# A hybrid GLA and RWKV-7 layer on one core: transfers planned to end later, the first 12 split weights read where they are made, row statistics spread by products with a repeated column

## The chip, the core and the metric

The kernel runs on one core of a Trainium2 chip. The core's engines each run their own queue in order: TensorE (PE in the profile, its weight loads PEld) multiplies matrices, VectorE (DVE) and ScalarE (ACT) work on tiles element by element, GpSimd (POOL) does the rest of such work, and SyncE (SP) issues the transfers, which 16 DMA engines carry out. Engines wait for each other by semaphores. The metric is the device time of one launch in microseconds (us).

## What is computed

One layer of a hybrid decoder: 4096 positions of width 1024, in float32. A projection of the normalised input feeds 4 heads of gated linear attention (GLA) and 8 heads of an RWKV-7 recurrence; their outputs, gated, go through one output projection, a residual add and a last normalisation.

```python
def _hybrid_layer(x, ...):
    h = _rmsnorm(x, norm_w)
    u = (h @ w_in).astype(f32)
    gla_u, rwkv_u = u[..., :GLA_IN], u[..., GLA_IN:]
    ...
    o = _gla_chunked(q, k, v, log_a)
    o = o * lax.rsqrt(jnp.mean(o * o, axis=-1, keepdims=True) + NORM_EPS) * gla_norm_w
    gla_out = o.reshape(B, T, GLA_VW) * jax.nn.silu(gg)
    ...
    y = _rwkv7_scan(r_h, decay, k_h, v_h, kk, a)
    y = (y - mu) * lax.rsqrt(var + RWKV_GN_EPS)
    rwkv_out = (y * rwkv_ln_w + rwkv_ln_b + bonus) * jax.nn.silu(rg)
    merged = jnp.concatenate([gla_out, rwkv_out], axis=-1)
    return x + merged @ w_out

x = _hybrid_layer(x, ...)
return _rmsnorm(x, final_norm_w)
```

## The kernel before

**Tiling.** Positions are taken in 8 blocks of 512 (b), features lie on the 128 partitions. A block needs 29 input weights of 1024 x 128: one for the two low-rank inputs (W_WA), for each of 4 pairs of RWKV heads four (W_R, W_RK, W_RV, W_RG), and 12 for GLA (W_K, W_Q, W_V, W_GG). The output projection has 8 more. Per block, rwkv_ab (L754) projects a pair of heads and builds the matrices of its 8 chunks of 64 positions (tiles De, Do, bk, Nb), rwkv_c (L909) walks the recurrence over the chunks with small products (tiles ch, sv, us, psd), rwkv_d (L951) normalises; gla_proj and gla_pair do GLA; out_block (L1137), and for the last block out_last (L1171), the output. There are 8 x 4 = 32 such RWKV units.

**Split weights.** Each float32 operand is written as a high and a low float16 part, and a product is three float16 products (high by high, high by low, low by high), so one weight costs 24 products of 128x128 by 512 columns. The weights are split on the chip in the first block, in the order of w_order (L581: W_WA, RK, R, then K, Q, then RV, RG, RK, then V, V and so on). split_w (L542) takes the absolute maximum of the raw weight on ACT (its elementwise result goes into the buffer hl, tiles wo, as scratch), spreads it over the partitions by a small product with ident (tile amW), makes a power of two of it on VectorE (tiles pw, scl, invs), and writes the high part on ACT and the low part on VectorE into hl. store_w (L560) stores hl to DRAM (wdr). There are two buffers hl, taken in turn. get_w (L525) loads a weight's two parts from wdr into a pair of tiles, wr for RWKV (4 tiles, so two pairs) or wg for GLA (3 tiles); the first block does so too.

**Row statistics.** A sum over the partitions comes out of stat_mm (L609) as rows: positions 128 g to 128 g + 127 in partition group g of 32. newton (L592) takes the inverse square root on VectorE (tiles nva, nta, nya, nyg, nyc). To spread a row over all partitions, bcast (L613) stores it to DRAM and loads it back repeated. At the two ends of the kernel spread (L625) is used in its place: it clears a tile rk on POOL, copies the four row groups into it on ACT, and multiplies by a constant sel. It is called in the first x_block, in the last rwkv_d and at the end of out_last.

**What sets the order.** Engine calls are recorded, not issued. Streams (generators for x, weights, recurrence and so on) hand their steps to a planner, which accounts each with a cost and builds a graph of steps (put, L196). forward (L230) and backward (L280) then simulate lists on the engines, and the steps are issued in the order of the planned starts. A transfer is planned with 0.63 us on SP's issue, 1.28 us until it starts, its bytes at 360 KB per us, and lag until others may use it: 1.6 us for a read from DRAM, 0.6 us for a write. A step that reuses a tile which a transfer reads follows 0.95 us after it. The output tensor counts as one DRAM tensor, so its stores follow each other in the plan. SP's queue is one for all transfers, and each DMA also waits for the one eight places earlier.

All engine calls go through one helper, so nearly all rows of the profile have its line, L364.

## Time and profile before

| | us |
|---|---|
| runs before: median of 3 | 2439.53 |
| lowest, highest | 2435.34, 2442.73 |
| the profiled execution | 2439.58 |
| its span, first to last instruction | 2437.8 |

The shares of that span: TensorE busy 94%, VectorE 70%, ACT 50%, POOL 35%; DMA engines 47% by the queues' packets. The page cuts the span into 40 slices of about 61 us; in the next lines each digit is the busy share of TensorE in a slice in tenths, then its granted clock, then the DMA engines' busy share.

```profile
PE   6799999999999999999999999999999999999996
PEclk9899999999999999999999999999999999999998
DMA  7775555454334553346433453346533454334431
```

Busy time of an engine does not add up over engines: a part of one engine's time matters where others wait for it. The lines on waits say who waited for whom; the chain follows the last instruction back to what released it.

### The profile page before, as it was taken

To read this page: it belongs to the slowest core of one execution; us is meant where nothing else is said; L and a number is where in the kernel's file an instruction comes from. 1 tells how busy PE (TensorE), PEld (TensorE's weight loads), DVE (VectorE), ACT (ScalarE), POOL (GpSimd) and SP (SyncE) were. 2 spreads that over 40 slices of the span, in tenths; PEclk is the share of its full clock that TensorE was granted. 3 is DMA by queue.
4 is the path that set the end of the run, shared out by engine and by line. 5 is a ranking of instruction groups with operands and counts; after the bars stand their busy time and mean duration, and the time that the engine had idled before them with its cause. 6 is when DMAs were issued, how large, how long until landed. Compare 5 with 4: busy or idle time off the path is not lost.

```text
span 2437.8 us, 54473 instructions
## 1 busy us (share of the span) xinstructions
PE 2292.0 (94%) x20684; PEld 1338.1 (55%) x20684; DVE 1696.4 (70%) x3866; ACT 1226.7 (50%) x3135; POOL 862.1 (35%) x2219
## 2 busy tenths in 40 slices
PE   6799999999999999999999999999999999999996
PEld 2456565455655555555564556555556455655652
DVE  7778778567675686757667667657867567576765
ACT  7456764454544555445544445445545455444342
POOL 3351434424334443335334153342433444323300
PEclk9899999999999999999999999999999999999998
DMA  7775555454334553346433453346533454334431
GB/s 226 241 249 181 169 152 149 111 166 142 90 109 117 171 146 96 97 122 185 120 94 109 136 178 112 99 120 184 137 98 103 122 163 130 109 98 119 143 90 64
DMA packets 278476, 331.91 MB, mean 136 GB/s; under 512 B 131540, under 2 KB 132804, under 8 KB 278212
## 3 DMA queue, kind: packets, MB, share of 16 engines
q1 hardware_dynamic: 278212, 328.42, 46.3%
q8 instruction: 162, 2.65, 0.5%
q14 instruction: 102, 0.84, 0.1%
HBM read 283.26 MB, written 45.05 MB: 135 GB/s over the span
## 4 chain that ended last, share of the span: by engine, by line
PE 48%; DVE 28%; DMA 11%; ACT 7%; issue 3%; SPq 2%; POOL 0%; DVEq 0%; ACTq 0%; POOLq 0%
PE bank L364 41%; PE ch L364 5%; DVE nta L364 3%; DVE bk L364 2%; DVE Nb L364 2%; DMA xr<-in_xT_dram 2%; DMA wdr<-wo 2%; DVE De L364 2%; DVE Do L364 2%; PE y L364 2%; SPq L364 2%; DVE cy L364 1%; DMA rn<-bcda 1%; DVE x L364 1%; ACT wo L364 1%
## 5 line engine op out<-in xcount | busy, mean ns | idle before, releaser
L364 PE MATMUL bank<-x,wr 128*128 128x512 f16 x3264 | 808.7, 381 | 12.1 <-DVE rgs L364 5.3
L364 POOL TENSOR_TENSOR tm<-Tc,f 128x60 f32<-128x60 f32 (+24 forms) x961 | 346.0, 360 | 711.1 <-DMA f<-nd 535.5
L364 PEld LDWEIGHTS <-wr 128*128 128x128 f16 x3264 | 308.0, 100 | 313.2 <-issue 24.7
L364 PE MATMUL bank<-x,wg 128*128 128x512 f16 x1536 | 386.2, 381 | 5.4 <-DMA wg<-wdr 4.8
L364 POOL TENSOR_TENSOR Tc<-Tc,tm 128x60 f32<-128x60 f32 (+24 forms) x961 | 343.8, 358 | 73.7
L364 PE MATMUL bank<-x,wo 128*128 128x512 f16 x1488 | 362.3, 381 | 0.5 <-ACT x L364 0.5
L364 DVE SCALAR_TENSOR_TENSOR sv<-ch,PC,psd 64x64 f32<-64x64 f32 x448 | 126.1, 281 | 207.2 <-PE ch L364 198.7
L364 POOL TENSOR_TENSOR xacc<-xacc,xr 128x512 f32<-128x512 f32 x98 | 132.0, 1347 | 371.2 <-ACT xr L364 224.6
L364 ACT ACTIVATE psd<-sv,PC 64x64 f32<-64x64 f32 x512 | 171.8, 342 | 137.5 <-DVE sv L364 130.8
L364 PEld LDWEIGHTS <-wg 128*128 128x128 f16 x1536 | 145.8, 100 | 154.5 <-issue 10.3
L364 PEld LDWEIGHTS <-wo 128*128 128x128 f16 x1488 | 141.2, 100 | 137.1 <-issue 4.4
L364 PEld LDWEIGHTS <-x 128*128 128x128 f16 x3120 | 188.7, 99 | 31.9 <-issue 12.0
L364 PE MATMUL bank<-wg,x 128*128 128x128 f16 x3072 | 202.7, 221 | 2.3 <-DMA wg<-wdr 1.4
L364 ACT COPY sv<-ch 64x64 f32<-64x64 f32 x512 | 105.0, 205 | 99.0 <-PE ch L364 91.8
L364 ACT ACTIVATE sa<-bank,mu_s 128x512 f32<-128x512 f32 x104 | 71.5, 687 | 130.9 <-PE bank L364 129.7
L364 PEld LDWEIGHTS ch<-us,Nb 128*128 128x128 f32 x512 | 87.7, 190 | 68.8 <-ACT us L364 54.4
L364 ACT COPY us<-ch 128x64 f32<-128x64 f32 x256 | 53.8, 210 | 140.4 <-PE ch L364 138.4
L364 POOL MEMSET Tc<- 32x8 f32 (+1 forms) x160 | 23.9, 150 | 277.1 <-DMA td<-Tc 261.3
L364 PEld LDWEIGHTS ch<-sv,bk 128*128 128x128 f32 x512 | 89.7, 190 | 47.8 <-ACT sv L364 31.8
L364 PE MATMUL ch<-us,Nb 128*128 128x64 f32 x512 | 94.4, 266 | 19.5 <-ACT us L364 17.8
L364 PE MATMUL ch<-sv,bk 128*128 128x128 f32 x512 | 105.5, 288 | 6.5 <-ACT sv L364 6.1
L364 PEld LDWEIGHTS ch<-sv,De 128*64 128x64 f32 x512 | 49.1, 135 | 97.3 <-issue 44.7
(323 smaller groups left out, 4111.0 us busy)
## 6 DMA issues: line engine op xcount, KB each, us to landing
wr<-wdr SPq DMA_DIRECT2D x272, 256.0 KB
wg<-wdr SPq DMA_DIRECT2D x192, 256.0 KB
xr<-in_xT_dram SPq DMA_DIRECT2D x176, 256.0 KB
wo<-wdr SPq DMA_DIRECT2D x128, 256.0 KB
wdr<-wo SPq DMA_DIRECT2D x37, 512.0 KB
f<-nd SPq DMA_DIRECT2D x128, 128.0 KB
x<-in_wt_dram SPq DMA_DIRECT2D x29, 512.0 KB
out_dram<-mgg SPq DMA_DIRECT2D x33, 256.0 KB
```

The costliest lines, as they stand in the source:

```text
L364: put(t0, self.name, d, lag, cols, tiles, tab, outs, ins, lambda: f(*a, **kw))
```

## The change

Five edits. **SPARE**: the plan's lag after a transfer, and the time after which a tile that a transfer reads may be reused, are 0.45 us longer in the graph that forward and backward order. **out**: the output tensor is left out of the planner's bookkeeping, so its stores no longer follow each other there. **ND**: the first 12 weights in w_order are split straight into a pair of wr or wg tiles, which get_w hands to the first block as they are; hl serves only as scratch for their maximum. They are stored to wdr from the pair, in two transfers of 256 KB in place of one of 512 KB, and not read back in the first block. A split may ask for its pair only once enough earlier weights have been asked for. **spread**: the ACT copies and the cleared tile go; each row group g (and head) is spread by a product of its own, whose weights are one column of sel repeated, with zeros outside the group's partitions; sel shrinks to 8 columns, filled by four small loads after a memset. **SN_**: the other set-up work starts one weight earlier.

```diff
@@ -23,6 +23,8 @@
 KT = 8
 TB = 512
 C = 64
+SPARE = 0.45
+ND = 12
 NW = {"r": 4, "g": 3, "o": 2}
 NSA = 1
 NXR = 2
@@ -37,7 +39,7 @@
 DL = 0.6
 WO_ = 6.0
 XN_ = 1
-SN_ = 3
+SN_ = 2
 XL = 0.05
 EL = 0.0
 PB = {"ch": 1, "y": 1}
@@ -99,7 +101,7 @@
     ready, used, busy = {}, {}, {}
 
     def parts(ap):
-        if ap.tensor.name.rsplit("_", 1)[0] in TABLES:
+        if ap.tensor.name == out.tensor.name or ap.tensor.name.rsplit("_", 1)[0] in TABLES:
             return []
         if ap.space == DRAM:
             return [(ap.tensor.name, 0)]
@@ -176,6 +178,8 @@
     last, turn = [None, 0], [0]
 
     def whole(ap):
+        if ap.tensor.name == out.tensor.name:
+            return []
         if ap.tensor.name.rsplit("_", 1)[0] in TABLES or ap.space == DRAM:
             return [(ap.tensor.name, 0)]
         return parts(ap)
@@ -202,7 +206,7 @@
         for k in ko:
             t0 = max(t0, rkey.get(k, 0.0))
         s = Step(len(steps), t0, eng, d, lag, cols, tiles, tab, f)
-        got = lambda m: m.lag - 0.1 * (m.eng == eng and eng in "VSG")
+        got = lambda m: m.lag + SPARE * (m.eng == "D") - 0.1 * (m.eng == eng and eng in "VSG")
         for k, timed in ki.items():
             rkey[k] = max(rkey.get(k, 0.0), t0)
             if k in wlast:
@@ -212,7 +216,7 @@
             if k in wlast:
                 s.follow(wlast[k], got(wlast[k]) if timed and eng != "T" else None)
             for m in readers.get(k, ()):
-                s.follow(m, (0.95 if m.eng == "D" else 0.1) if timed else None)
+                s.follow(m, (0.95 + SPARE if m.eng == "D" else 0.1) if timed else None)
             wlast[k], readers[k] = s, []
         for k in ki:
             if k not in ko:
@@ -439,8 +443,11 @@
     c64 = sb(one, [P, 64], F32, "c64")
     smask = sb(one, [P, TB], U8, "smask")
     gmask = sb(one, [P, TB], U8, "gmask")
-    sel = sb(one, [P, P], F32, "sel")
-    D.dma_start(sel, ck[:, CK_SEL:CK_SEL + P])
+    sel = sb(one, [P, 4, 2], F32, "sel")
+    G.memset(sel, 0.0)
+    for g in range(4):
+        q = slice(32 * g, 32 * g + 32)
+        D.dma_start(sel[q, g, :], ck[q, CK_SEL:CK_SEL + P:64])
     ident = sb(one, [P, P], F32, "ident")
     make_identity(nc, ident)
     uh = [sb(one, [P, 512], F16, f"uh{i}") for i in range(2)]
@@ -516,22 +523,28 @@
     woinv = sb(one, [P, KT], F32, "woinv")
     nwx = sb(one, [P, 10], F32, "nwx")
 
-    split_done = set()
+
+    split_done, first, made, got = set(), {}, dict(r=0, g=0), dict(r=0, g=0)
+    pair = lambda st: [sb(wp, [P, KT, P], F16, "w" + st, NW[st]) for _ in range(2)]
 
     def split(src, sc, h, l):
         S.activation(h, src, AF.Copy, scale=sc)
         V.scalar_tensor_tensor(l, src, sc, h, ALU.mult, ALU.subtract)
 
     def get_w(i, st="g"):
+        if st != "o":
+            got[st] += 1
         if i not in split_done:
             yield lambda: i in split_done
+        if i in first:
+            return first.pop(i)
         if st == "o":
             if done["W"] < NWT + KT:
                 yield lambda: done["W"] == NWT + KT
             w = wot()
             w = [w[:, 0], w[:, 1]]
         else:
-            w = [sb(wp, [P, KT, P], F16, "w" + st, NW[st]) for _ in range(2)]
+            w = pair(st)
         for a in range(2):
             D.dma_start(w[a], wdr[i][a])
         return w
@@ -544,7 +557,16 @@
         junk = hl.rearrange("p a k t -> p (a k t)").bitcast(F32).rearrange("p (k t) -> p k t", k=KT)
         iv = invs[:, i:i + 1]
         yield from absmax_scale(raw, scl[:, i:i + 1], iv, "W", junk)
-        split(raw, scl[:, i:i + 1], hl[:, 0], hl[:, 1])
+        w = [hl[:, 0], hl[:, 1]]
+        if n < ND:
+
+            st = "r" if i < W_Q else "g"
+            k = made[st]
+            made[st] += 1
+            if got[st] < k + (st == "g"):
+                yield lambda: got[st] >= k + (st == "g")
+            w = first[i] = pair(st)
+        split(raw, scl[:, i:i + 1], *w)
         V.tensor_scalar(iv, iv, nwx[:, 9:10], 0.125 if W_Q <= i < W_K else 1.0, ALU.mult, ALU.mult)
         if W_R <= i < W_RG or i == W_WA:
             j = i - 1 if i else 12
@@ -555,7 +577,13 @@
             if i >= W_GG:
                 h = i - W_GG
                 V.tensor_tensor(gnh[:, h:h + 1], hinv[:, i:i + 1], pkt[:, PK_GN:PK_GN + 1], ALU.mult)
-        store_w(i, hl)
+        if n < ND:
+            for a in range(2):
+                D.dma_start(wdr[i][a], w[a])
+            split_done.add(i)
+            done["W"] += 1
+        else:
+            store_w(i, hl)
 
     def store_w(i, hl):
         D.dma_start(wdr[i].rearrange("a p k t -> p a (k t)"), hl.rearrange("p a k t -> p a (k t)"))
@@ -622,15 +650,12 @@
             D.dma_start(o[n * h:n * h + n], d[h:h + 1].rearrange("h g t -> h (g t)").broadcast_to((n, TB)))
 
 
-    def spread(rows, ps):
-
-        d = sb(rt, [P, TB], F32, "rk")
-        G.memset(d, 0.0)
+    def spread(rows, ps, heads):
+
+        n = P // heads
         for g in range(4):
-            q_ = slice(32 * g, 32 * g + 32)
-            S.copy(d[q_, P * g:P * g + P], rows[q_])
-        yield after(d)
-        T.matmul(ps, lhsT=sel, rhs=d, start=True, stop=True)
+            for h in range(heads):
+                T.matmul(ps[n * h:n * h + n, P * g:P * g + P], lhsT=sel[:, g, h:h + 1].broadcast_to((P, n)), rhs=rows, start=True, stop=True)
 
     def pbank(tag):
         return sb(psp, [P, TB], F32, tag, PB[tag])
@@ -686,7 +711,8 @@
         y = newton(ps[:, 0:P], 1.0 / DM, 1e-6, None, "g")
         if b == 0:
             rb = yield from need("X")
-            yield from spread(y, rb)
+            yield after(y)
+            spread(y, rb, 1)
         else:
             rel("X")
             rb = sb(rt, [P, TB], F32, "xacc")
@@ -956,7 +982,8 @@
         st = newton(pst[:, 0:P], 1.0 / 64, 64e-5, None, "c")
         if b == NB - 1 and p == 3:
             rs = yield from need("d")
-            yield from spread(st, rs)
+            yield after(st)
+            spread(st, rs, 2)
         else:
             rel("d")
             bcast(st, 2, rs, "c")
@@ -1220,7 +1247,8 @@
             rel("o")
         rs = newton(pst[:, 0:P], 1.0 / DM, 1e-6, None, "g")
         pb = yield from need("o")
-        yield from spread(rs, pb)
+        yield after(rs)
+        spread(rs, pb, 1)
         for n in range(KT):
             V.scalar_tensor_tensor(part[n], part[n], pkt[:, PK_FN + n:PK_FN + n + 1], pb, ALU.mult, ALU.mult)
             D.dma_start(out[P * n:P * n + P, TB * b:TB * b + TB], part[n])
```

Three places in the order, where the prediction's steps rest. The first is SP's queue behind the eight loads of x (mgg, mgr), before; x_1_0 to x_1_3 are the raw weights, pkt the packed vectors, f, crs and glr raw low-rank weights.

```order
L364 DMA x_1_0_0_80<-in_wt_dram 128x1024
L364 DMA pkt_95<-in_pk_dram 128x60
L364 DMA sel_102<-in_ck_dram 128x128
L364 DMA x_1_1_0_81<-in_wt_dram 128x1024
L364 DMA x_1_2_0_82<-in_wt_dram 128x1024
L364 DMA f_0_214<-in_wg_dram 128x8x16
L364 DMA crs_215<-in_wua_dram 64x512 x2
L364 DMA glr_216<-in_wua_dram 64x512 x2
L364 DMA x_1_3_0_83<-in_wt_dram 128x1024
```

The same place now:

```order
L368 DMA pkt_95<-in_pk_dram 128x60
L368 DMA sel_102<-in_ck_dram 32x2x1 x2
L368 DMA x_1_0_0_80<-in_wt_dram 128x1024
L368 DMA x_1_1_0_81<-in_wt_dram 128x1024
L368 DMA f_0_214<-in_wg_dram 128x8x16
L368 DMA crs_215<-in_wua_dram 64x512
L368 DMA sel_102<-in_ck_dram 32x2x1 x2
L368 DMA crs_215<-in_wua_dram 64x512
L368 DMA glr_216<-in_wua_dram 64x512 x2
L368 DMA x_1_2_0_82<-in_wt_dram 128x1024
```

The first raw weight has moved behind pkt and two of the four loads of sel, the third and fourth raw weight behind crs and glr.

The second is ACT's queue behind the squares of x, before; wo are the buffers hl, amW the maximum, nyg the first normalisation's row, mgg and mgr the tiles of x.

```order
L364 ACTIVATE wo_136,amW_208<-x_1_0_0_80 128x1024
L364 ACTIVATE wo_137,amW_209<-x_1_1_0_81 128x1024
L364 COPY rk_192<-nyg_206 32x128 x3
L364 ACTIVATE wo_136<-x_1_0_0_80,scl_176 128x1024
L364 COPY rk_192<-nyg_206 32x128
L364 ACTIVATE wo_137<-x_1_1_0_81,scl_176 128x1024
L364 CAST x_0_0_0_76<-mgg_0_84 128x512
L364 CAST x_0_1_0_77<-mgg_0_86 128x512
```

And now:

```order
L368 ACTIVATE wo_136,amW_208<-x_1_0_0_80 128x1024
L368 ACTIVATE wo_137,amW_209<-x_1_1_0_81 128x1024
L368 ACTIVATE wr_210<-x_1_0_0_80,scl_176 128x1024
L368 CAST x_0_0_0_76<-mgg_0_84 128x512
L368 CAST x_0_1_0_77<-mgg_0_86 128x512
L368 CAST x_0_0_0_76<-mgg_0_85 128x512
L368 CAST x_0_1_0_77<-mgg_0_87 128x512
L368 CAST x_0_2_0_78<-mgg_0_88 128x512
```

The four copies rk are gone, and the high part of the first weight is written to wr_210, the tile that TensorE multiplies from; the second weight's high part has moved behind the casts of x.

The third is VectorE's queue where the first unit's bk gets its second half, behind the inverse norm rn, before; wo_136 and wo_137 with x_1 are the low parts of split weights.

```order
L364 SCALAR_TENSOR_TENSOR wo_136<-x_1_2_0_82,scl_176,wo_136 128x1024
L364 TENSOR_REDUCE amW_208<-bank_0_180 128x1
L364 TENSOR_SCALAR pw_201<-amW_208 128x1
L364 TENSOR_SCALAR pw_201<-pw_201 128x1
L364 TENSOR_SCALAR scl_176<-pw_201 128x1
L364 SCALAR_TENSOR_TENSOR rn_193<-rk_192,pkt_95,rn_193 128x512
L364 SCALAR_TENSOR_TENSOR ta_195<-ta_195,rn_193 128x512
L364 TENSOR_TENSOR De_0_128<-rn_193,EP_230 64x8x64
L364 TENSOR_TENSOR Do_0_130<-rn_193,EP_230 64x8x64
L364 SCALAR_TENSOR_TENSOR bk_238<-ta_195,E_194 64x8x64 x2
L364 SCALAR_TENSOR_TENSOR wo_137<-x_1_3_0_83,scl_176,wo_137 128x1024
```

And now:

```order
L368 SCALAR_TENSOR_TENSOR wg_227<-x_1_0_0_80,scl_176,wg_229 128x1024
L368 TENSOR_REDUCE amW_208<-bank_0_181 128x1
L368 SCALAR_TENSOR_TENSOR r_197<-r_197,pkt_95,kf_196 128x512
L368 TENSOR_SCALAR pw_203<-amW_208 128x1
L368 SCALAR_TENSOR_TENSOR rn_193<-rk_192,pkt_95,rn_193 128x512
L368 SCALAR_TENSOR_TENSOR ki_239<-bank_0_180,invs_118,gbc_223 128x512
L368 SCALAR_TENSOR_TENSOR ta_195<-ta_195,rn_193 128x512
L368 TENSOR_TENSOR De_0_128<-rn_193,EP_230 64x8x64
L368 TENSOR_TENSOR Do_0_130<-rn_193,EP_230 64x8x64
L368 SCALAR_TENSOR_TENSOR bk_237<-ta_195,E_194 64x8x64 x2
L368 TENSOR_SCALAR pw_203<-pw_203 128x1
```

The split in the first row is the seventh weight's before and the fifth weight's now, so two fewer stand ahead of bk; the low part goes to wg_227. The GLA step ki has moved in among the products with rn.

## Prediction

> **What bounds the kernel now.** I read the page first, then busy time by stretch, then who makes TensorE wait, then the chain of waits at both ends.
>
> ```profile
> span 2437.8 us, 54473 instructions
> PE 2292.0 (94%) x20684; PEld 1338.1 (55%) x20684; DVE 1696.4 (70%) x3866; ACT 1226.7 (50%) x3135; POOL 862.1 (35%) x2219
> ```
>
> TensorE is the bound: it is busy 94% of the span, so all its idle time is 2437.8 - 2292.0 = 145.8 us. The busy time by stretch (columns: stretch and its length, then PE, PEld, DVE, ACT and POOL busy with counts, granted clock, DMA share, GB/s) says where it lies.
>
> ```profile
> 0.00:28.18 28.18, 11.59 (x78) 5.08 (x79) 17.34 (x60) 17.19 (x29) 12.18 (x33) 1.00 0.85 265
> 28.18:79.70 51.52, 36.09 (x173) 14.99 (x173) 41.68 (x109) 34.45 (x64) 15.45 (x17) 0.93 0.67 222
> 60.00:90.00 30.00, 18.25 (x86) 10.15 (x85) 25.63 (x54) 12.04 (x21) 5.92 (x5) 0.77 0.73 241
> 79.70:140.00 60.30, 52.25 (x452) 35.26 (x453) 44.52 (x109) 28.18 (x51) 26.43 (x62) 0.92 0.70 217
> 240.00:2340.00 2100.00, 2026.59 (x18535) 1187.16 (x18534) 1459.76 (x3233) 1044.38 (x2746) 782.00 (x2035) 0.99 0.45 129
> ```
>
> The first 140 us hold 16.6 + 15.4 + 8.1 = 40.1 us of idle TensorE, the 2100 us in the middle only 73.4 (3.5%). Whatever starts the projections sooner shifts all that follows, because from 240 us on TensorE has work nearly all the time. The waits of TensorE in the first 140 us (total, times, longest) and the chain there (start, length, what) name the cause.
>
> ```profile
> PE bank L364 <- ACT wo L364: 18.5, 9, 7.0
> PE bank L364 <- DMA wg<-wdr: 3.8, 1, 3.8
> ...
> 18.92 6.58 DMA wdr<-wo
> 25.66 1.16 ACT wo L364 x2
> 26.86 0.81 PE bank L364 x2
> 30.03 6.37 DMA wdr<-wo
> 74.07 5.22 DMA wdr<-wo
> ```
>
> A split weight is stored to DRAM from one of two buffers wo; the absolute maximum of the weight after next is taken on ACT with that buffer as scratch, so it waits until the store has landed, and the small product that spreads the maximum stands in TensorE's queue ahead of everything else. That is the 18.5 us.
>
> **The change: first weights.** The first 12 weights are split straight into wr and wg, where the projections read them. The wait on the store and the read back from DRAM (24 transfers of 256 KB) go; wo stays as scratch alone. What is late next is VectorE. Rows of the head:
>
> ```profile
> 4.50 0.43 SPq L364 DMA_DIRECT2D x<-in_wt_dram  x1
> 7.09 0.98 SPq L364 DMA_DIRECT2D x<-in_wt_dram  x2
> 14.61 0.91 ACT L364 COPY rk<-nyg 32x128 f32<-32x128 f32 x3 [0.41 <-DVE scl L364]
> 15.54 1.15 ACT L364 ACTIVATE wo<-x,scl 128x1024 f16<-128x1024 f32 x1
> 16.71 0.29 ACT L364 COPY rk<-nyg 32x128 f32<-32x128 f32 x1
> 17.11 2.04 PE L364 MATMUL bank<-rk,sel 128*128 128x512 f32 x2 [0.36 <-issue]
> 28.18 2.74 PE L364 MATMUL bank<-x,wr 128*128 128x512 f16 x6 [0.53 <-DMA wr<-wdr]
> 50.18 2.33 PE L364 MATMUL bank<-x,wr 128*128 128x512 f16 x10
> 65.28 0.49 PE L364 MATMUL bank<-ident,amW 128*128 128x128 f32 x2 [4.02 <-ACT wo L364]
> 73.13 0.49 PE L364 MATMUL bank<-ident,amW 128*128 128x128 f32 x2 [0.41 <-ACT wo L364]
> 79.70 0.79 PE L364 MATMUL bank<-De,bk 64*128 64x128 f32 x2 [2.41 <-DVE bk L364]
> 80.40 1.28 DVE L364 SCALAR_TENSOR_TENSOR wo<-x,scl,wo 128x1024 f16<-128x1024 f32 x1
> ...
> PE bank L364 <- ACT wo L364: 9.1, 3, 7.0
> ```
>
> I follow the work to the first pairing products (De with bk), at 79.70 now. They waited 2.41 us for VectorE, so its queue decides. (a) The start: the four row copies on ACT, with a weight's piece between them, keep the spread product from 14.61 to 17.11, 2.5 us. But the first raw weight is now issued after pkt and two pieces of sel, in the slot that today issues at 7.09 instead of 4.50, and its ACT pass stands ahead of the casts; I give 1.2 us back and keep 1.3. (b) In VectorE's order seven splits stand ahead of the first bk that needs rn; in the new order five. Two splits of 1.28 us go behind: 2.6 us. Moved, not saved, but later TensorE has other work to cover them. (c) From 28.18 to 79.70 VectorE idles 51.52 - 41.68 = 9.8 us, for ACT, which waits for stores, or for TensorE. All of it or none may go; I take half, 4.9. Together 8.8, bounds 3.9 and 13.7. (d) Of the 18.5 us of waits 9.1 lie before 60 us (the last row above) and 4.02 + 0.41 before 79.70; 5.0 are left after it, most for weights beyond the twelfth, which still go through wo; I take 1.5, bounds 0 and 5.0. (e) Between 60 and 90 us the granted clock is 0.77 with TensorE busy 18.25: at full clock that work is 18.25 x 0.23 = 4.2 us shorter. I take 2.0, bounds 0 and 4.2. The head is 8.8 + 1.5 + 2.0 = 12.3, bounds 3.9 and 22.9.
>
> Two rules of the Trainium skill speak to this. The row of a 512 KB store is 6.58 or 6.37 us; DMA: Bandwidth & Descriptors, section Anatomy of one DMA, fits about 2.0 us plus bytes over 436 GB/s, an estimate of 3.2 us here (fitted on another issuing path), by which the wait removed were half as long and the head some 6 us poorer. The row decides: the queues are loaded (DMA share 0.85). TensorE: Matmul & The Clock Gate, Part 1, says an idle window of about 3.4 us halves the clock and a busy one restores it; by it, thin early products run cold, so an earlier start buys less than its length. The trace agrees: 2.74 us for six products at 28.18, 0.46 each, against 0.22 where TensorE is dense (2.33 for ten at 50.18).
>
> The new cover to lose: a split weight's wr pair may be rewritten only when both of its stores have landed. SP issues them in order, each behind the split it stores, and the raw loads, the mask constants and bcda queue behind them; VectorE waits for the last. If that binds, the wait on a store returns in another place (first rival). SN_ from 3 to 2 moves a few small operations of the set-up one weight earlier; SP gets three more tiny loads of sel and 12 more stores in place of 24 loads. Hidden under the 2 MB of x at the start; costed at nothing beyond (a).
>
> **The change: the tail.** Rows:
>
> ```profile
> 2404.01 1.22 ACT L364 COPY rk<-nyc 32x128 f32<-32x128 f32 x4 [5.64 <-DVE nyc L364]
> 2405.37 2.05 PE L364 MATMUL bank<-rk,sel 128*128 128x512 f32 x2 [4.39 <-ACT rk L364]
> 2426.07 1.23 ACT L364 COPY rk<-nyg 32x128 f32<-32x128 f32 x4 [3.41 <-DVE nyg L364]
> 2427.40 1.74 PE L364 MATMUL bank<-rk,sel 128*128 128x512 f32 x2 [4.26 <-issue]
> ...
> 85.00 1.11 PE L364 MATMUL bank<-ident,bk 128*128 128x128 f32 x4
> 96.80 0.60 PE L364 MATMUL bank<-ident,bk 128*128 128x128 f32 x4
> ```
>
> Both copies lie bare on the last chain, with some 0.1 us of semaphore each: 1.22 + 1.23 + 0.2 = 2.65 us go. The products: four records at 85.00 and 96.80 are two float32 products of 128 columns (each is two passes), 1.11 at the slow clock and 0.60 at the fast. Four cost 2.2 or 1.2; now 2.05 and 1.74. For two heads there are eight, 64 wide: 2.2 if the halves run side by side, 4.4 if not. I take 2.2 for both: +0.15 and +0.46, so the tail gains 2.0, bounds 0.1 less (loss, one after another) and 3.9 (side by side, fast).
>
> **The change: planned ends.** SPARE adds 0.45 us to the time at which the planner lets anyone use a transfer, and out no longer chains its stores in the plan. No instruction is added; the order changes nearly everywhere.
>
> ```profile
> DVE bv L364 <- DMA bv<-bcdb: 31.6, 18, 4.8
> DVE cy L364 <- DMA crs<-bcdc: 27.8, 15, 4.0
> DVE rn L364 <- DMA rn<-bcda: 18.9, 15, 4.3
> ACT xr L364 <- DMA xr<-in_xT_dram: 27.6, 23, 3.6
> ...
> 2221.99 2.31 DMA bcdc<-nyc
> 2225.97 4.17 DMA crs<-bcdc
> ...
> PE ch L364 <- ACT us L364: 16.5, 26, 1.8
> ```
>
> The plan's numbers give a small store 1.28 + 0.01 + 0.6 = 1.9 us and a 128 KB load 1.28 + 0.36 + 1.6 = 3.2; the chain shows 2.31 and 4.17. So the plan is optimistic by about 1.4 us a round trip, and SPARE closes 0.9 of it. From 240 to 2340 us DVE and ACT stand behind such transfers 31.6 + 27.8 + 18.9 + 27.6 = 105.9 us. But TensorE's 73.4 us there go to many causes, the largest the recurrence (16.5 for us), and hardly to a transfer directly. I take 3 us, since most of those waits are covered; a new order over 20,000 products may as well cost or gain 10.
>
> **Sum.** 12.3 + 2.0 + 3.0 = 17.3 us off the profiled execution's 2439.58 us (span 2437.8), which is the median of the runs shown (2439.53) within 0.05: 2422.
>
> **Rivals.** *The wait comes back on the pairs* (chance 0.25): the split waits for the pair's stores instead of for wo's. For it: SP's chain above is in order and a store takes 5 to 6.6 us. Against: the order lets TensorE's first weight product wait for ACT alone. Head 3.9, tail 2.0, plan 0: 2433.7.
>
> *Everything fits* (0.18): VectorE's idle 9.8 us goes, clock and later waits too, tail 3.9, plan 6: 18.6 + 3.9 + 6 = 28.5, 2411.
>
> *The recurrence starves* (0.07), the other side: planned 0.45 us later, projections are packed behind loads and no longer fill the gaps between a recurrence's steps, where TensorE already waits for us (16.5 us in 26 waits). There are 32 units of 8 steps, 256 in all; head and tail are worth 14.3 us, so it decides from 14.3 / 256 = 0.056 us a step. At 0.1 a step: 2439.6 - 14.3 + 25.6 = 2451. Against: 26 waits in 256 steps leave nine steps in ten without any.
>
> **How the numbers follow.** The forecast has 0.50. What a measurement here can tell from no change is about 0.3%, 7.3 us: below 2432.3 is faster, above 2446.9 slower. Forecast (nearly all of it) and "everything fits" lie below, the first rival at 2433.7 with about a third below, the slow one above for most of its chance: 0.75, 0.20, 0.05. The range 2406 to 2437 takes in the first rival with 3 us beyond it and most of the good case, and leaves out the starved recurrence.
>
> **What would show it.** Right: no TensorE wait on ACT wo before 60 us, first projection product near 20 us, De with bk near 70, granted clock over 0.9 from 60 to 90, no copies rk at the end and the last two spread products at 2.2 us or less, idle from 240 to 2340 within 10 us of 73. Wrong: SP or ACT waiting for wdr<-wr stores before 80 us (first rival), TensorE's waits for us, sv and ch up by tens of us (third), or eight narrow products at over 4 us.

## Result and profile after

| | before | after |
|---|---|---|
| median of 4 runs each, us | 2440.64 | 2421.56 |
| lowest, highest, us | 2435.34, 2442.73 | 2420.10, 2425.58 |
| the profiled execution, us | 2439.58 | 2425.58 |
| its span, us | 2437.8 | 2423.8 |

The ratio is 0.9934, with a 95% interval from 0.9914 to 0.9954: faster, by 19 us in the medians and by 14.0 us between the two profiled executions. The forecast was 2422. The number came true, and so did the signs that were named for it, but for one small wait; the experiments below do not bear out the sizes given to its parts, the tail excepted. One execution of experiment 8, its profiled one (7752.36 us), and one of the kernel before beside experiments 5 to 8 (5310.17 us) were disturbed, and the ratios leave them out.

First the span and the engines' busy times of the changed kernel, from its page.

```profile
span 2423.8 us, 54428 instructions
PE 2301.9 (95%) x20710; PEld 1344.5 (55%) x20710; DVE 1691.6 (70%) x3866; ACT 1219.0 (50%) x3123; POOL 851.4 (35%) x2217
```

TensorE's idle time is 2423.8 - 2301.9 = 121.9 us, 23.9 less than before. But its busy time rose by 9.9 us for the same projections and nearly the same small products. Both halves of that sum matter later. The busy time by stretch (columns as before):

```profile
0.00:28.18 28.18, 13.82 (x90) 6.87 (x91) 18.83 (x64) 16.26 (x25) 15.12 (x34) 1.00 0.77 245
28.18:79.70 51.52, 45.96 (x244) 22.75 (x242) 45.22 (x123) 37.22 (x71) 13.99 (x16) 0.97 0.54 171
60.00:90.00 30.00, 25.63 (x184) 15.31 (x182) 25.26 (x64) 18.08 (x31) 4.83 (x4) 0.94 0.73 228
79.70:140.00 60.30, 54.20 (x514) 37.32 (x513) 45.31 (x119) 33.93 (x60) 27.47 (x67) 0.92 0.70 215
140.00:240.00 100.00, 92.22 (x823) 54.99 (x819) 78.90 (x222) 69.75 (x164) 34.84 (x96) 0.91 0.67 204
240.00:2340.00 2100.00, 2035.06 (x18576) 1189.59 (x18574) 1459.97 (x3239) 1039.11 (x2739) 759.95 (x2006) 0.99 0.45 129
```

TensorE now idles 14.4, 5.6 and 6.1 us in the first three stretches that don't overlap, where it idled 16.6, 15.4 and 8.1. From 60 to 90 us the granted clock is 0.94 against 0.77. So the head looks as forecast. The next stretch does not: from 140 to 240 us the old kernel had this row, better in busy time and in clock.

```profile
140.00:240.00 100.00, 94.14 (x894) 58.64 (x893) 80.89 (x234) 68.53 (x149) 25.50 (x72) 0.97 0.70 219
```

Busy time by granted clock is roughly the work done at full clock: 94.14 x 0.97 = 91.3 us before, 92.22 x 0.91 = 83.9 after. That is less work than before in the same stretch; whether the lead is lost there is followed further down. In the middle the idle time fell from 73.4 to 64.9 us. TensorE's waits in the first 140 us of the changed kernel (total, times, longest):

```profile
PE bank L368 <- DVE bk L368: 10.4, 3, 6.0
PE bank L368 <- ACT rk L368: 4.5, 1, 4.5
PE bank L368 <- ACT x L368: 3.1, 2, 1.9
PE bank L368 <- DVE amW L368: 2.5, 1, 2.5
PE bank L368 <- ACT wo L368: 1.3, 1, 1.3
```

Of the 18.5 us for ACT wo 1.3 are left, at 12.9 us, for the first maximum itself and not for a store; VectorE's bk is late next, as the prediction said. The marks in the timeline: the first projection product, the first of De with bk, the two spread products of the tail, and the last run of output products between them.

```profile
19.32 0.58 PE L368 MATMUL bank<-x,wr 128*128 128x512 f16 x1 [1.88 <-ACT x L368]
...
66.14 0.49 PE L368 MATMUL bank<-De,bk 64*128 64x128 f32 x2 [4.14 <-DVE bk L368]
...
2392.00 1.09 PE L368 MATMUL bank<-nyc,sel 128*64 128x128 f32 x16 [2.14 <-DVE nyc L368]
...
2400.28 7.34 PE L368 MATMUL bank<-x,x 128*128 128x512 f16 x23 [0.20 <-DVE x L368]
2412.55 2.07 PE L368 MATMUL bank<-nyg,sel 128*128 128x128 f32 x8 [2.90 <-DVE nyg L368]
```

The first product is 8.9 us earlier than before (19.32 against 28.18), De with bk 13.6 us (66.14 against 79.70). The copies to rk are gone, and the spread products take 1.09 and 2.07 us.

Every sign that the prediction named is there, but for that one wait of 1.3 us before 60. Whether the signs are the cause is another question: the three edits were made together, and the planner wrote the whole program in a new order.

### The profile page after: what moved, and what is told of

The parts are those of the page before. It is cut to its first block, busy times and chain, and to the rows that moved or that the text cites. A ratio compares the mean times of both kernels' runs of the same rounds, so it can differ in the third digit from the quotient of the medians.

```text
span 2423.8 us, 54428 instructions
## 1 busy us (share of the span) xinstructions
PE 2301.9 (95%) x20710; PEld 1344.5 (55%) x20710; DVE 1691.6 (70%) x3866; ACT 1219.0 (50%) x3123; POOL 851.4 (35%) x2217
## 4 chain that ended last, share of the span: by engine, by line
PE 63%; DVE 22%; DMA 6%; ACT 5%; issue 2%; SPq 1%; POOL 1%; DVEq 0%; ACTq 0%; POOLq 0%
PE bank L368 56%; PE ch L368 6%; DVE nta L368 2%; PE y L368 2%; DVE bk L368 2%; DVE Nb L368 2%; DVE De L368 1%; DVE Do L368 1%; DVE mgg L368 1%; DVE mgr L368 1%; DMA bv<-bcdb 1%; DVE gbc L368 1%; SPq L368 1%; DVE cy L368 1%; DVE sv L368 1%
## 5 line engine op out<-in xcount | busy, mean ns | idle before, releaser
L368 POOL TENSOR_TENSOR tm<-Tc,f 128x60 f32<-128x60 f32 (+24 forms) x961 | 338.5, 352 | 661.7 <-DMA f<-nd 405.5
L368 POOL MEMSET Tc<- 32x8 f32 (+1 forms) x160 | 23.6, 148 | 318.2 <-DMA td<-Tc 303.5
```

Of the source, the lines that this page charges most:

```text
L368: put(t0, self.name, d, lag, cols, tiles, tab, outs, ins, lambda: f(*a, **kw))
```

## Experiments

Each kernel below was timed beside the kernel before on the same chip, whose median was 2439.67 us in the runs of experiments 1 to 4, 2439.26 in 5 to 8 and 2438.03 in 9 to 12. Differences from 2421.6 compare these runs with those of the changed kernel, which stood beside a median of 2440.64. The ratios take that out: by them experiment 1 lies 10 us below the changed kernel (8 by the medians), 2 lies 13 above (15), 3, 8 and 10 lie 10, 9 and 8 below (7, 7 and 9). The changed kernel's own ratio has an interval of 5 us to either side, so differences of 7 to 10 us are only just clear of noise.

**Experiments 1 to 4: one part undone, one part alone.**

1, no first weights:

```diff
-ND = 12
+ND = 0
```

SN_ stays at 2 here.

> The changed kernel with ND = 0: every weight is split into wo and stored, none straight into wr or wg; the planned ends and the new spread stay. Theory A (each part is worth its own term; the head is worth what TensorE's idle time up to 240 us lost, 12.1 us): 2421.6 + 12 = about 2434 us; De with bk back to about 79 us, waits for ACT wo back to about 18 us, TensorE's idle time from 240 to 2340 us within 5 us of the 64.9 of the changed kernel. Theory B (the gain was the new order in the middle, by planned ends): within 4 us of 2421.6. Theory C (the earlier start is paid back at a slow clock between 80 and 240 us): about 2428, with the granted clock from 140 to 240 us back at 0.97.

Measured: 2413.4 us, ratio 0.9894 (0.9871 to 0.9917). Without the edit that was to bring 12 us the kernel is not 12 us slower but 8 faster; its runs (2411.6 to 2418.8) don't overlap those of the changed kernel. The next row, of its timeline, shows that the edit is really out: the first long run of projections waits 8.66 us for a load of wr from DRAM. The row after it is the middle, by stretch.

```profile
28.65 6.66 PE L368 MATMUL bank<-x,wr 128*128 128x512 f16 x19 [8.66 <-DMA wr<-wdr]
```

```profile
240.00:2340.00 2100.00, 2046.90 (x18708) 1197.92 (x18706) 1473.51 (x3252) 1052.83 (x2780) 786.88 (x2034) 1.00 0.46 130
```

TensorE idles 41.1 us up to 240 us (33.8 in the changed kernel), as theory A wants, and 53.1 us in the middle (64.9). So by idle time the head loses 7.3 us, and the middle gives 11.8 back. A and C fall; B isn't shown by this run alone.

2, the planner of before:

```diff
-SPARE = 0.45
+SPARE = 0.0
...
-        if ap.tensor.name == out.tensor.name or ap.tensor.name.rsplit("_", 1)[0] in TABLES:
+        if ap.tensor.name.rsplit("_", 1)[0] in TABLES:
...
-        if ap.tensor.name == out.tensor.name:
-            return []
```

> The changed kernel with SPARE = 0 and the stores of out chained in the plan again: first weights and new spread stay, the planner is that of before. Theory A: 3 us slower, 2424.6, and the head keeps its gain (De with bk near 66 us). Theory B: most of the gain is lost, 2433 or more, with TensorE idle 73 us or more from 240 to 2340. Theory D (an order is worth whatever it happens to be worth): anything within 10 us of 2421.6, faster as likely as slower, with the difference in the middle and no single wait that carries it.

Measured: 2436.35 us, ratio 0.9987 (0.9972 to 1.0002). With first weights and new spread both in, the gain is gone but for 3 us (none to 7 by the interval), though De with bk starts at 64.16 us, earlier than in the changed kernel. Its middle idles 74.2 us:

```profile
240.00:2340.00 2100.00, 2025.77 (x18565) 1189.71 (x18566) 1462.82 (x3245) 1042.41 (x2727) 767.89 (x2015) 0.99 0.45 128
```

That is what theory B expected, and it rules out that the early start alone made the 19 us.

3, the old spread:

```diff
...
-            for h in range(heads):
-                T.matmul(ps[n * h:n * h + n, P * g:P * g + P], lhsT=sel[:, g, h:h + 1].broadcast_to((P, n)), rhs=rows, start=True, stop=True)
+            q_ = slice(32 * g, 32 * g + 32)
+            S.copy(d[q_, P * g:P * g + P], rows[q_])
+        yield after(d)
+        T.matmul(ps, lhsT=sel, rhs=d, start=True, stop=True)
...
```

> The changed kernel with the old sel, the copies to rk and one product of 512 columns at the three places. Theory A: 2 to 4.5 us slower (tail 3.2 by the rows of the two traces, start 1.3): 2424 to 2426; from the end of the last nyc to cy 3.5 us against 1.26, from the end of the last nyg to mgg 3.2 against 2.25. Theory D: the tail's own rows do that, but the total is anywhere within 10 us of it, since the whole order moves.

Measured: 2414.66 us, ratio 0.9895 (0.9871 to 0.992). With the new spread taken out the kernel is 7 us faster. The copies are back on its chain (1.22 and 1.23 us on ACT), so the edit did what it says; the total moved the other way, which only theory D allows.

4, first weights alone in the kernel before (SN_ = 2 goes with them, since the first units wait for the set-up):

```diff
+ND = 12
...
-SN_ = 3
+SN_ = 2
```

> The kernel before with ND = 12 (and SN_ = 2, which ND needs) alone: old spread, old planner. Theory A: 12 us faster than before, about 2428; De with bk at 66 to 69 us (the 1.3 us of the spread are missing). Theory B: within 4 us of before. Theory D: 2418 to 2438, with De with bk at 66 to 69 in any case.

Measured: 2434.06 us, ratio 0.9971 (0.9956 to 0.9987): 5.6 us by the medians, 7 by the ratio, with an interval from 3 to 11. De with bk starts at 73.37 us, 6.3 earlier than before, where 66 to 69 was expected.

**Experiments 5 to 8: the planned ends, and their size.**

5, planned ends alone in the kernel before:

```diff
+SPARE = 0.45
...
-        if ap.tensor.name.rsplit("_", 1)[0] in TABLES:
+        if ap.tensor.name == out.tensor.name or ap.tensor.name.rsplit("_", 1)[0] in TABLES:
```

> The kernel before with the planned ends alone (SPARE = 0.45 and out left out of the plan's keys), without first weights and with the old spread. Theory P (the planned ends carry the gain, by shorter waits of VectorE and ACT for DMA from 240 to 2340 us and so less idle TensorE there; the first weights and the spread add next to nothing on top): 2414 to 2420 us, TensorE idle in that stretch 53 to 65 us against 73.4 before, DVE and ACT waiting for DMA there 95 to 115 us against 145.4 before. Theory D (each order is worth what it happens to be worth): anywhere from 2412 to 2440, with no relation to those waits. Theory A (my prediction's terms): 2437.

Measured: 2443.04 us, ratio 1.0014 (1.0003 to 1.0025). Theory P falls as it was stated. The planner did what it was told: VectorE and ACT wait 104.5 us for DMA between 240 and 2340 (all rows of that view added; 145.4 before), and TensorE idles 69.5 us there. But TensorE's busy time is 10.1 us longer than before, for the same products, and its idle time only 4.0 shorter.

6, SPARE = 0 with out still free:

```diff
-SPARE = 0.45
+SPARE = 0.0
```

> The changed kernel with SPARE = 0, and out still left out of the plan's keys. If the 0.45 us carries the planned ends: about 2434, like the run with both undone (2436.35), TensorE idle 70 to 75 us from 240 to 2340. If the stores of out carry them: about 2421. Theory D: between or outside these, by 8 us.

Measured: 2421.26 us, ratio 0.9935 (0.9919 to 0.9951), the changed kernel's own time, with waits of VectorE and ACT for DMA back at 141.3 us. By the rule written down before, the stores of out carry the planned ends; but with experiment 5 against it (out free there too, and no gain) that is no more shown than the 0.45. Against shorter waits for DMA as what makes the time speak both runs: here the waits are long and the time is short, there it is the other way about.

7, twice the spare time:

```diff
-SPARE = 0.45
+SPARE = 0.9
```

> The changed kernel with SPARE = 0.9: a store and the load behind it then end 1.8 us later in the plan, past the 1.4 us by which the plan was short in the last round trip of the profile before. Theory P: waits for DMA of DVE and ACT from 240 to 2340 fall below 100 us; the time stays between 2412 and 2422, since work planned later than it could start costs TensorE something too. Third rival of the prediction (the recurrence starves): slower than 2430, with TensorE's waits for us and sv above 25 us. Theory D: anywhere from 2412 to 2432.

Measured: 2461.82 us, ratio 1.0095 (1.008 to 1.011), slower than before by 1%, though the waits for DMA are the lowest of all (90.0 us) and TensorE idles only 55.4 us in the middle. The page, and TensorE's wait for us from 240 to 2340:

```profile
span 2458.8 us, 54428 instructions
...
PE 2326.3 (95%) x20710; PEld 1354.5 (55%) x20710; DVE 1690.7 (69%) x3866; ACT 1223.0 (50%) x3123; POOL 858.3 (35%) x2217
```

```profile
PE ch L368 <- ACT us L368: 8.0, 14, 1.4
```

The recurrence does not starve (8.3 us for us in the changed kernel), so the third rival's mechanism is not this. Against the changed kernel 24.4 of the 35.0 us are busy time, for as many products, and 10.6 idle time (20.0 more at the two ends, 9.5 less in the middle). The mean granted clock is 0.973 against 0.982: that is at most 0.009 x 2440 = 22 us, so the clock can be most of the 24.4.

8, nearly the same spare time:

```diff
-SPARE = 0.45
+SPARE = 0.4
```

> The changed kernel with SPARE = 0.40 in place of 0.45: by its meaning next to no change, but a new order. It measures what a new order alone is worth. If orders scatter little: within 4 us of 2421.6. Theory D: 5 to 12 us away from it, on either side; with theory P as well, on the side of 2413 to 2422 rather than 2434.

Measured: 2414.37 us, ratio 0.9899 (0.9883 to 0.9914), its other four runs within 2413.8 and 2414.6. An edit of 0.05 us in the plan goes with 7 to 9 us, though the intervals of the two ratios touch at 0.9914. No profile of this kernel is read here.

**Experiments 9 to 12: the order held, and the order alone.** In 9 to 11 the planner still sees the steps of the kernel that is named, and only what is issued at some of the steps is another.

9, the new spread in the order of before:

```diff
...
+        emit[0] = lambda: None
         G.memset(d, 0.0)
...
             S.copy(d[q_, P * g:P * g + P], rows[q_])
+        emit[0] = None
         yield after(d)
-        T.matmul(ps, lhsT=sel, rhs=d, start=True, stop=True)
+        emit[0] = products
+        T.matmul(ps, lhsT=sel[:, 0, 0:1], rhs=d, start=True, stop=True)
...
```

> The kernel before, its order held: the planner still plans the old spread, but at the places of its copies nothing is issued and at the place of its product the four or eight products with the repeated column; the rest stands word for word as before. So this is the new spread without a new order. Theory A (prediction's terms, re-measured by rows): the tail 2 to 3.3 us, the start 0 to 2.5 us shorter: 2434 to 2437. If the time saved is covered elsewhere: 2439.5. Theory D says the same as A here, since the order doesn't change: no more than 6 us either way.

Measured: 2437.52 us, ratio 0.9995 (0.9983 to 1.0008): within what can be told from none. The profiles, in the same order, tell more. First the kernel before, then this one.

```profile
2396.97 1.68 PE L364 MATMUL bank<-x,x 128*128 128x512 f16 x7
...
2414.53 6.57 PE L364 MATMUL bank<-x,x 128*128 128x512 f16 x23 [0.20 <-DVE x L364]
```

```profile
2394.30 1.68 PE L366 MATMUL bank<-x,x 128*128 128x512 f16 x7
...
2401.30 1.86 PE L644 MATMUL bank<-nyc,sel 128*64 128x128 f32 x16 [2.99 <-DVE nyc L366]
...
2410.34 7.47 PE L366 MATMUL bank<-x,x 128*128 128x512 f16 x23 [0.20 <-DVE x L366]
...
2422.72 2.08 PE L644 MATMUL bank<-nyg,sel 128*128 128x128 f32 x8 [2.89 <-DVE nyg L366]
```

From the seven products to the end it is 2437.8 - 2396.97 = 40.8 us before and 2433.5 - 2394.30 = 39.2 here: the tail is 1.6 us shorter, where 2.0 was predicted, although the last 23 products in it take 0.9 us longer. The rows by stretch say why they do. First the kernel before, then experiment 9, over just these 23 products; the granted clock is the third number from the end.

```profile
2414.53:2421.10 6.57, 6.57 (x27) 2.54 (x30) 4.71 (x7) 3.60 (x6) 0.00 (x0) 0.78 0.00 0
```

```profile
2410.34:2417.81 7.47, 7.47 (x27) 2.78 (x30) 4.84 (x7) 3.62 (x6) 0.00 (x0) 0.68 0.01 3
```

6.57 x 0.78 = 5.1 and 7.47 x 0.68 = 5.1: the same work at two clocks.

10, the same on the kernel of experiment 3, which makes it the changed kernel's three parts in another order:

> The run with the old spread in the changed kernel (2414.66), its order held, with the new spread issued in the places of the old. All three parts of the change are in it, as in the changed kernel (2421.6); only the order is another. Theory D (the 7 us between these two were the order's, not the spread's): 2410 to 2413. If the new spread itself costs time in the changed kernel: 2418 or more.

Measured: 2412.44 us, ratio 0.9903 (0.9889 to 0.9918), 2.2 us under experiment 3, and 9.1 us under the changed kernel with the same parts. From a newton step of the last nyc to the end it is 0.9 us shorter than in experiment 3 (2411.7 - 2374.37 = 37.3 us against 2412.6 - 2374.40 = 38.2), though the 23 products take 1.2 us longer. First experiment 3, where they run at full clock, then this one:

```profile
2390.20:2395.32 5.12, 5.12 (x27) 2.21 (x30) 4.49 (x7) 3.56 (x6) 0.00 (x0) 1.00 0.00 0
```

```profile
2390.00:2396.36 6.36, 6.36 (x27) 2.50 (x30) 4.71 (x7) 3.60 (x6) 0.00 (x0) 0.80 0.01 3
```

11, a third split buffer in the order of before (the scratch of the maximum is half as wide too):

```diff
...
+    spare = [t.bitcast(F16).rearrange("p (k t) -> p k t", k=KT) for t in mfree["r"][3:5]]
...
+        hi, lo = [(hls[0][:, 0], hls[0][:, 1]), (hls[1][:, 0], hls[1][:, 1]), spare][n % 3]
...
```

> The kernel before, its order held, but the 29 input weights take turns on three split buffers (the third in two tiles that lie idle then), and the scratch of the absolute maximum is half as wide. So the wait for the store goes without a new order, and the weights still go through DRAM. Theory A (the wait on the store is worth my head terms c, d and e, 8.4 us): about 2431, waits of TensorE for ACT wo below 6 us, De with bk at 72 to 76. If the wait is covered by what is late next (VectorE, the read back, or a slow clock): 2437 to 2440, with De with bk less than 3 us earlier. If all of the 18.5 us goes: 2421.

Measured: 2434.14 us, ratio 0.9988 (0.9976 to 1.0001): by the ratio 0.0012 x 2438 = 3 us, between 6 and none. ACT's wait for the stores in the first 140 us was this before, and has no row any more:

```profile
ACT wo L364 <- DMA wdr<-wo: 25.4, 10, 4.4
```

TensorE still waits 7.3 us for the maxima (5.0 for ACT mgr, which is the third buffer, and 2.3 for ACT wo; 18.5 before). In place of the rest it waits for what comes next, the read back from DRAM, and De with bk moves from 79.70 to 78.76 us:

```profile
PE bank L366 <- DMA wg<-wdr: 6.3, 1, 6.3
PE bank L366 <- ACT mgr L507: 5.0, 1, 5.0
...
PE bank L366 <- DMA wr<-wdr: 3.6, 2, 2.2
```

```profile
78.76 0.49 PE L366 MATMUL bank<-De,bk 64*128 64x128 f32 x2 [1.59 <-DVE bk L366]
```

The wait that carried the forecast of the head is worth about 3 us, none to 6, when it alone is taken away and the order stays.

12, a change of order with no meaning, in the kernel before:

```diff
-                        d, lag, cols, tiles = n / 2400 + 0.0025, 0.25, n * r.shape[0] / 128, k
+                        d, lag, cols, tiles = n / 2400 + 0.0025, 0.26, n * r.shape[0] / 128, k
```

> The kernel before with 0.26 us in place of 0.25 as the plan's time from a product's end to its reader: no change of meaning, but another order. Theory D: 3 to 12 us from 2439.5, on either side; the kernel before is then one draw among such orders. If orders scatter little: within 2 us.

Measured: 2442.46 us, ratio 1.0021 (1.0006 to 1.0036). The kernel before is one draw too, though not an unlucky one by this neighbour.

All runs side by side; idle times in us from the rows by stretch (length less busy time), busy time and clock (the mean granted one) are those of the one profiled execution, not of the median. P says whether the planned ends were in (o: out alone), F the first weights, S the new spread; the sign h marks a part put in with the order held.

| run | F | P | S | median | idle to 240 | 240 to 2340 | 2340 to end | busy | clock |
|---|---|---|---|---|---|---|---|---|---|
| before | - | - | - | 2440.6 | 45.9 | 73.4 | 26.4 | 2292.0 | 0.983 |
| after | F | P | S | 2421.6 | 33.8 | 64.9 | 23.2 | 2301.9 | 0.982 |
| 1 | - | P | S | 2413.4 | 41.1 | 53.1 | 21.9 | 2300.9 | 0.984 |
| 2 | F | - | S | 2436.4 | 40.6 | 74.2 | 23.6 | 2296.3 | 0.982 |
| 3 | F | P | - | 2414.7 | 36.4 | 59.0 | 18.8 | 2298.4 | 0.984 |
| 4 | F | - | - | 2434.1 | 37.2 | 69.9 | 26.9 | 2295.3 | 0.983 |
| 5 | - | P | - | 2443.0 | 41.8 | 69.5 | 30.6 | 2302.1 | 0.981 |
| 6 | F | o | S | 2421.3 | 40.4 | 66.7 | 21.0 | 2285.6 | 0.986 |
| 7 (0.9) | F | P | S | 2461.8 | 43.0 | 55.4 | 34.0 | 2326.3 | 0.973 |
| 8 (0.4) | F | P | S | 2414.4 | | | | | |
| 9 | - | - | h | 2437.5 | 43.4 | 76.6 | 22.6 | 2290.9 | 0.984 |
| 10 | F | P | h | 2412.4 | 36.5 | 61.5 | 17.5 | 2296.2 | 0.988 |
| 11 | - | - | - | 2434.1 | 40.8 | 75.9 | 26.2 | 2293.6 | 0.982 |
| 12 | - | - | - | 2442.5 | 38.9 | 80.7 | 27.3 | 2294.1 | 0.982 |

Two things can be read from it. With planned ends TensorE idles 53.1 to 69.5 us in the middle, without them 69.9 to 80.7 (the means of six runs each are 60.6 and 75.1; experiment 6 is left out). And the time does not follow that column: experiments 5 and 7 have the planned ends and are no faster than before, because the other columns, busy time and the two ends, move as much.

Two more readings change the picture. First, busy time by clock, the work at full clock, sorts the kernels too: with planned ends it is 2258 to 2269 us (after 2301.9 x 0.982 = 2260), without them 2252 to 2256 (before 2292.0 x 0.983 = 2253), in experiment 6 2254. So the plan with spare time idles less in the middle and is busy some 9 us longer, for reasons that no run here shows. Second, in pairs that differ in the plan alone or nearly so, planned ends go with 15 us less (2 and after), 19 less (4 and 3) and 24 less (9 and 1, which differ in SN_ and in how the spread was put in as well), and with 2.4 more only where nothing else is changed (before and 5, by the table). All six kernels with the plan of before lie between 2434 and 2443 us, and of the eight whose planner leaves out free six lie between 2412 and 2422; experiments 5 and 7 do not. That the plan gains with either other edit, and that experiment 5 drew a poor order, is an account as good as that of order alone. A few neighbours of experiment 5 (0.44 or 0.46 us) would have told them apart; they were not run.

The marks in the traces follow the lead over the kernel before to its end. A mark is the first De with bk of a unit; these are the first, sixth and last of the 32 units, and the end of the span.

| lead over before, us | first unit | sixth | last | end |
|---|---|---|---|---|
| after | 13.6 | 14.0 | 20.4 | 14.0 |
| 1 (no first weights) | 9.0 | 3.3 | 22.5 | 20.8 |
| 2 (planner of before) | 15.5 | 5.1 | 2.2 | 3.1 |
| 4 (first weights alone) | 6.3 | 2.6 | 8.4 | 8.6 |
| 6 (SPARE = 0) | 16.0 | 2.8 | 21.3 | 24.1 |

The last mark, before and after:

```profile
2293.85 0.49 PE L364 MATMUL bank<-De,bk 64*128 64x128 f32 x2 [0.84 <-DVE bk L364]
```

```profile
2273.41 0.48 PE L368 MATMUL bank<-De,bk 64*128 64x128 f32 x2 [0.23 <-DVE bk L368]
```

At the last mark the changed kernel and experiments 1 and 6 are within 2.1 us of each other. They part behind it, between that mark and the seven products with which the tail begins: before, after, experiment 1, experiment 6.

```profile
2293.85:2396.97 103.12, 96.34 (x895) 57.87 (x895) 65.71 (x195) 39.31 (x120) 6.68 (x25) 0.95 0.35 93
2273.41:2384.49 111.08, 100.50 (x891) 60.19 (x891) 64.74 (x193) 39.45 (x120) 7.59 (x29) 0.91 0.33 87
2271.33:2377.33 106.00, 97.31 (x891) 58.63 (x890) 64.48 (x191) 39.37 (x120) 4.26 (x18) 0.94 0.34 91
2272.51:2376.51 104.00, 96.56 (x892) 57.70 (x892) 65.66 (x193) 39.17 (x120) 5.37 (x22) 0.95 0.34 93
```

It is the same work (busy time by clock 91.5, 91.5, 91.5 and 91.7), but the changed kernel takes 8.0 us longer over it than the kernel before, 4.2 of them at a lower clock and 3.8 idle; the tail gives 1.5 back. So of the 6.8 us by which experiment 1's profiled execution beats the changed kernel's, 5.1 arise there, some 2200 us behind the place of the first weights. These are single executions.

## Why the prediction was right, and where it was not

- **Right: what bounds it, and all signs but a small one.** First projection near 20 us (19.32), De with bk near 70 (66.14), clock over 0.9 from 60 to 90 (0.94), no copies at the end, spread products under 2.2 us (1.09 and 2.07), idle time in the middle within 10 us of 73 (64.9). Only one short wait for wo, 1.3 us, is left before 60 where none was said. The first rival, a wait for the pairs, did not come: neither ACT nor VectorE has a row of waiting for a store from wr or wg in the first 140 us, nor SP before 80. GpSimd has one (tm, 18.6 us), where before it had one of 31.3 us for the read back.
- **The head, 12.3 us: the mark came true, the step from there to the end failed.** The mark moved 13.6 us, where (a) to (c) gave 8.8 with an upper bound of 13.7. The busy time up to it says of what that is made (before, then now; VectorE's is the third busy time):

```profile
0.00:79.70 79.70, 47.68 (x251) 20.07 (x251) 59.02 (x168) 51.63 (x92) 27.63 (x49) 0.95 0.74 237
```

```profile
0.00:66.14 66.14, 46.46 (x255) 21.28 (x255) 51.18 (x145) 46.16 (x82) 26.32 (x47) 1.00 0.63 200
```

  VectorE idles 20.7 us ahead of the mark before and 15.0 now: 5.7 us less, where (a) and (c) gave 6.2. Its work ahead of the mark is 7.8 us less, where (b) gave 2.6. So more than half of the 13.6 us is work that moved behind the mark, which (b) took as covered later. "Seen at De with bk" was counted as "gained at the end", and the table of marks does not bear that out: with leads of 15.5 and 16.0 us at the first mark the end is 3.1 and 24.1 us early. In the changed kernel the 14.0 us of the sixth unit are also those of the end, by 6.4 us won on the way and as much lost behind the last mark. In time, taking the store's wait away with the order held is worth 3 us (experiment 11, none to 6), the whole edit alone 5.6 (experiment 4, 3 to 11). Beside the other two edits its removal gains 8 us (experiment 1), and put beside the planned ends alone it goes with 28 us less (experiments 5 and 3). No one size fits these; the order moves with the edit each time.
- **The clock,** named in (e) for 60 to 90 us only, is 0.91 against 0.97 before between 140 and 240. With first weights it is 0.88 to 0.93 there in experiments 2, 4, 6 and 7 too, but 0.97 and 0.95 in 3 and 10. The Trainium skill's TensorE: Matmul & The Clock Gate, Part 1, says that an idle window of about 3.4 us halves the clock; the prediction drew from it that an earlier start buys less than its length, and left that out of the sum. The lower clock would fit, but in the changed kernel the marks show no lead lost for good (14.0 us at the sixth unit), and no run shows thin early products as the reason.
- **The tail, 2.0 us: right.** 1.6 us by rows with the order held (experiment 9), 0.9 on another order (experiment 10). From the seven products to the end the new spread takes 37.2 to 39.7 us in six profiles (39.3 in the changed kernel), the old one 40.8 to 42.0 in four. In sum too little to be seen in a time. The parts were off both ways: narrow products run side by side (1.09 and 1.86 us for eight, where 2.2 was taken), and in experiments 9 and 10 the 23 products after them ran 0.9 and 1.2 us longer, at a lower clock.
- **The plan, 3.0 us give or take 10: mis-sized, as far as the runs tell.** I called it a small gain with noise about it. Undoing it alone costs 15 us (13 by the ratios), at or beyond that bound; adding it alone costs 4 (experiment 5, within 0.14%). Its reason, transfers planned too early, is real in the waits (145.4 to 111.7 us for DMA on VectorE and ACT from before to after), but experiment 6 has waits of 141.3 us and the same time.
- **The order.** Orders of the same work, or with edits that mean nothing, lie 4 (experiment 12), 7 (experiment 8) and 9 us (experiment 10) apart. The parts alone give 5.6, -3.8 and about 0.5 us, 2 us in all; together they give 19. The 17 us between may belong to the order that came out of the three together, or to the plan, which gains only beside another edit; the runs do not part the two. No run gives the terms of 12.3 and 3.0 us their sizes, so that the sum of 17.3 met 19.1 is in large part luck.
- **The third rival** did not come, and its mechanism was not what made 0.9 slow; by one profile most of that can be the clock.
- **Small slips in the working,** without effect on the forecast: ten products in 2.33 us are 0.23 us each, not 0.22; the upper bound of the tail comes to 4.0 us rather than 3.9; and the 18.6 us for the head in "everything fits" is not worked out from the terms. The six products at 28.18, 0.46 us each, were read as cold; the granted clock is given as 1.00 there (28.18 to 30.92), but the trace's clock entries begin only at 31.6 us, and the twelve products at 32.48 take 0.23 us each. So a slow clock fits them but is not recorded.

What stays open: what made the 19 us, the planned ends in company or the order; which property of an order sets busy time and clock; and whether 0.45 or the free stores matter, since experiment 6 has the time without the 0.45 and experiment 5 has both without the time. Of the 9.9 us more busy time from before to after the mean clock explains 0.001 x 2440 = 2.4; the rest goes with the longer work that all kernels with spare time in the plan show, and its reason is open.

The best kernel measured is experiment 10, ratio 0.9903; experiments 1, 3 and 8 cannot be told from it. It was picked from several orders, so it says little of its parts.

## What to carry to other kernels

Where a planner writes the whole order, time an edit also with the order held, and time a few edits that mean nothing, around each single edit too: the scatter among them, here 4 to 9 us in 2440, is the least that an edit must bring before its reason is believed. Before you call edits useless or lucky, read all pairs of runs that differ in one of them. A mark that arrives earlier is not yet a gain: ask how much work only moved behind it, and follow the lead from mark to mark until it reaches the end or is gone. And read TensorE's time as idle plus busy time: fewer waits with a lower clock can lose.

## What the runs showed of the hardware

- One program runs at different mean clocks from one execution to the next. The six runs of experiment 6 have granted clocks from 0.979 (2427.21 us, the slowest) to 0.986 (2415.48 us, the fastest, which is the profiled one), the twelve of experiment 2 from 0.977 (2444.59, the slowest) to 0.986 (2432.58, the fastest). So busy times of single profiles carry this scatter. Between orders it goes further: the five runs of experiment 7 lie between 0.973 and 0.976, those of experiment 10 between 0.983 and 0.988, with 20710 matmul records each.
- Eight float32 products of 128 columns onto 64 partitions each, sixteen records, took 1.09 us in three profiles (after, experiments 6 and 10) and 1.57 to 1.97 in four; the granted clock was 1.00 at 1.09 us and 0.54 at 1.86. By the prediction's row of 0.60 us for two full-width products, eight in a row would take 2.4 at full clock: the halves run side by side. In the changed kernel's trace the records start in pairs, 6 to 7 ns apart, a pair every 109 ns.
- The last 23 output products are 5.0 to 5.1 us of work at full clock in each of ten profiles, and took from 5.12 us at a granted clock of 1.00 (experiment 3) over 6.57 at 0.78 and 7.34 at 0.69 to 7.76 at 0.65 (experiment 1). Up to 2.6 us of the end hang on the clock in them. In experiment 3 no wait of TensorE in the 18 us ahead of them is longer than 2.3 us; in the kernel before there are waits of 4.4, 3.8 and 1.7 us. The Trainium skill's TensorE: Matmul & The Clock Gate, Part 1, says that the window which restores the clock runs freely and that the cold stretch varies with its phase; that fits these ten, and by it the 0.9 and 1.2 us above need not be the spread's doing.
